# Second stages of the Hyena transforms as plain fp32 products, in a DeepNorm hybrid encoder layer

## The chip, the core and the metric

The kernel runs on one core of one Trainium2 chip. The metric is the device time of one execution in microseconds (us). The engines are TensorE (PE for matmuls, PEld for its weight loads), VectorE (DVE), ScalarE (ACT), GpSimd (POOL) and SyncE (SP, which here only issues DMAs). Each engine works through its own instructions in a fixed order and waits on semaphores.

## The reference

One post-norm layer over `x` of 1 x 1024 x 1024: an adaLN-modulated LayerNorm, one combined input projection of 9216 columns, then two branches, dilated window attention (512 channels) and a Hyena operator of order 2 (512 channels), gates, an output projection and a second LayerNorm. The change concerns the Hyena branch, whose core is this:

```python
def bidirectional_long_conv(z, h_fwd, h_bwd):
    L, C = h_fwd.shape
    circ = jnp.concatenate([h_fwd, jnp.zeros((1, C), jnp.float32), h_bwd[:0:-1]], axis=0)
    hf = jnp.fft.rfft(circ, axis=0)
    zf = jnp.fft.rfft(z.astype(jnp.float32), n=2 * L, axis=1)
    y = jnp.fft.irfft(zf * hf[None], n=2 * L, axis=1)[:, :L]
    return y.astype(z.dtype)
...
    z = v
    for o, gate_o in enumerate((x1, x2)):
        z = gate_o * (bidirectional_long_conv(z, filters[:, o, 0], filters[:, o, 1]) + filt_bias[o] * z)
    y_hy = z * jax.nn.silu(g_hy)
```

## The kernel before, in words

Everything is fp32 in meaning. Most matmuls use the faster type fp32r on operands split into a high and a low part, and add up three products: high by high, high by low, low by high. The input projection is the bulk of TensorE's work: `proj` (L234) splits one 1024 x 128 block of `w_in` into `wh` and `wl` (ACT at L222, POOL at L223) and runs 2 x 24 matmuls of 128x512 at L242 against the split input `hTh`, `hTl`. There are 64 such projections; those of the gates (`gate_r`, twelve of them "early") and of later channels serve as fill work on TensorE wherever the Hyena stages leave room.

The Hyena stages take the transform of length 2048 in two steps. `stage1` (L462) does butterflies over 16 residues on DVE with tiles of the ring `pair()` (tag `f`, seven buffers) and yields, one after the other, eight operands `y` of 128 x 2 x 256: `j = -1` for the two real residues and `j = 0..6` for the others. The second stage multiplies each `y` by a 128 x 128 table of cosines and one of sines; that is `split_product` (L492). It casts `y` to `yh` (ACT L499), forms the rest `yl` (DVE L500), writes negated copies of one half (ACT L511 and L512), and runs six fp32r matmuls of 128x512 at L521, with tables that are split as well; for `j = -1` in the filter stage twelve of 128x256 at L509:

```python
            ACT.copy(yh[:, c, :], y)
            V.tensor_tensor(yl[:, c, :], y, yh[:, c, :].bitcast(F32), ALU.subtract)
            ACT.mul(yh[:, n, :], y[:, at, :], -1.0)
            ACT.mul(yl[:, n, :], yl[:, 2 * at, :].bitcast(F32), -1.0)
            for k, (m, v) in enumerate(ops):
                PE.matmul(z, m, v, start=k == 0, stop=k == 5)
```

Two stages use it. `gen_filter` (L534) runs four times: eight blocks `g` of the filter in time (matmuls L560 and L561, times a decay table `dk` loaded at L556, product on DVE at L563), butterflies at L566 to L569, `stage1`, eight products with `tabf`, a copy by ACT (`hs`, L573, two buffers) and a DMA to `h_dram` (L581). `long_conv` (L615) also runs four times, under high priority: `stage1` of the data, eight forward products with `tcon` (j = -1: four fp32 matmuls with `tcon0` at L531, unsplit already), on DVE the product with the spectrum `ht` loaded from `h_dram` (`p1`, `p2` at L625 to L634), the inverse product, and butterflies back. `conv_to_rows` (L583) prepares its inputs: a projection, a width-3 convolution on DVE (L608) and eight transposes (L612).

A scheduler sets the order on each engine at build time, from dependencies, buffer counts and its own costs; on the chip the order is fixed. Buffers of one tile are in rings; a write waits until the ring's oldest buffer has been read. The right-hand pools `fl3` (with `tabf`) and, after it, `hy` and `hy2` (with `tcon`, `ht`) use the same memory one after the other.

Of the kernel before, what the change touches and what calls it, by code (L numbers as in the profile page):

```python
# [54 lines left out]
def _split(t):  # L55

    def r12(x):
        m, e = np.frexp(x)
        return np.ldexp(np.round(m * 4096) / 4096, e)

    h = r12(t)
    return h.astype(np.float32), r12(t - h).astype(np.float32)


def _dft_tables():

# [6 lines left out]
    flt = np.zeros((P, 36, P), np.float32)  # L73
    con = np.zeros((P, 28, P), np.float32)
    con0 = np.zeros((P, 8, P), np.float32)
    for n, j in enumerate(RES):
        m = b[:, None] * j + 16 * b[:, None] * k2[None, :]
        th = 2 * np.pi * (m % NB) / NB
        for i, t in enumerate((np.cos(th), np.sin(th))):
            flt[:, 4 * n + 2 * i], flt[:, 4 * n + 2 * i + 1] = _split(t)  # L80
        th = 2 * np.pi * ((m + j * k2[None, :]) % NB) / NB
        for i, t in enumerate((np.cos(th), np.sin(th))):
            con[:, 4 * n + 2 * i], con[:, 4 * n + 2 * i + 1] = _split(t)
    k = np.arange(64)
    alt = np.where(B_OF_P % 2 == 0, 1.0, -1.0)
    for i, k1 in enumerate((0, 8)):
# [8 lines left out]
        for m, (f, v) in enumerate(((c, ci), (sn, si))):  # L95
            t = 28 + 4 * m + 2 * i
            flt[:, t, rows], flt[:, t + 1, rows] = _split(f)
            con0[:, 2 * m + i, rows] = f
            con0[rows, 4 + 2 * i + m] = v.T
# [68 lines left out]
def hybrid_encoder(ctx, tc, A):  # L168
# [102 lines left out]
    with ExitStack() as st:  # L271
# [168 lines left out]
        tabf = fl3.tile([P, 36, P], F32R, name="tabf")  # L440
        PO.dma_start(tabf, A["t_flt"])
# [50 lines left out]
        def split_product(j, y, tab, inverse, pool):  # L492
# [3 lines left out]
            yh, yl = [pool.tile([P, 3, W], F32R, name="y" + q, tag="y" + q, bufs=2) for q in "hl"]  # L496
            at = int(inverse)
            c, n = slice(at, at + 2), 2 - 2 * at
            ACT.copy(yh[:, c, :], y)  # L499
            V.tensor_tensor(yl[:, c, :], y, yh[:, c, :].bitcast(F32), ALU.subtract)  # L500
            if j < 0:
                for i in range(2):
                    ops = []
                    for q in range(2):
                        t = 28 + 4 * i + 2 * q
                        for m, v in ((t, yh), (t, yl), (t + 1, yh)):
                            ops.append((tab[:, m, :], v[:, q, :]))
                    for k, (m, v) in enumerate(ops):
                        PE.matmul(z[:, i, :], m, v, start=k == 0, stop=k == 5)  # L509
                return z  # L510
            ACT.mul(yh[:, n, :], y[:, at, :], -1.0)  # L511
            ACT.mul(yl[:, n, :], yl[:, 2 * at, :].bitcast(F32), -1.0)  # L512
            ops = []
            for i, lo in ((0, at), (1, 1 - at)):
# [666 lines left out]
```

## Time and profile before

| | us |
|---|---|
| median of 3 runs (range) | 1463.67 (1461.36 to 1464.23) |
| the profiled execution | 1466.4 |
| its span, first to last instruction | 1464.6 |
| filter stage, first filter product to first product of a long convolution | 141.3 to 302.3 |
| four long convolutions, to the last inverse product | 302.3 to 613.9 |
| TensorE busy by the page | 1351.3 |
| VectorE busy | 957.6 |
| ScalarE busy | 624.4 |

The busy time of PE in the page counts the whole duration of each matmul, in which its neighbours overlap; how long TensorE is held by one matmul is read from the distance between two starts. A wait is charged to the instruction that waited and to the one that ended the wait. The rows come further down.

### The profile page before, as it was taken

To read this page: it belongs to the slowest core of one execution; us is meant where nothing else is said; L and a number is where in the kernel's file an instruction comes from. 1 tells how busy PE (TensorE), PEld (TensorE's weight loads), DVE (VectorE), ACT (ScalarE), POOL (GpSimd) and SP (SyncE) were. 2 spreads that over 40 slices of the span, in tenths; PEclk is the share of its full clock that TensorE was granted. 3 is DMA by queue.
4 is the path that set the end of the run, shared out by engine and by line. 5 is a ranking of instruction groups with operands and counts; after the bars stand their busy time and mean duration, and the time that the engine had idled before them with its cause. 6 is when DMAs were issued, how large, how long until landed. Compare 5 with 4: busy or idle time off the path is not lost.

```text
span 1464.6 us, 18389 instructions
## 1 busy us (share of the span) xinstructions
PE 1351.3 (92%) x6707; PEld 1098.4 (75%) x6707; DVE 957.6 (65%) x1709; ACT 624.4 (43%) x1220; POOL 282.2 (19%) x160
## 2 busy tenths in 40 slices
PE   4788979889899999999999999999999999689997
PEld 1467767767777777788988788878887888567886
DVE  4798768767999898745156714761466144288866
ACT  1544444534244443446355534663466343242110
POOL 1221121210113122141121112111211111231220
PEclk9799999999999999999999999999999999899999
DMA  9633544332112222121113421311131114588523
GB/s 255 182 97 105 175 133 149 110 130 79 54 58 69 87 65 79 58 84 30 44 59 116 103 61 58 92 30 43 59 91 31 44 58 123 184 249 220 158 88 72
DMA packets 157024, 145.86 MB, mean 100 GB/s; under 512 B 16611, under 2 KB 126591, under 8 KB 156678
## 3 DMA queue, kind: packets, MB, share of 16 engines
q1 hardware_dynamic: 156486, 140.44, 32.7%
q0 software_dynamic: 288, 4.19, 0.8%
q8 instruction: 53, 0.87, 0.3%
q14 instruction: 37, 0.30, 0.1%
q10 hardware_dynamic: 160, 0.06, 0.0%
HBM read 116.73 MB, written 27.92 MB: 99 GB/s over the span
## 4 chain that ended last, share of the span: by engine, by line
PE 64%; DVE 11%; DMA 5%; ACT 3%; issue 2%; POOL 1%; SPq 0%; DVEq 0%; ACTq 0%; POOLq 0%
PE pj L242 33%; PE pj L888 6%; PE z L521 6%; PE po L1138 6%; PE pj L1103 4%; PE po L929 2%; PE pp L922 2%; DVE iv L447 2%; DVE f L447 1%; DMA dk<-in_t_dec 1%; DMA wor<-in_w_out 1%; PE z L531 1%; PE ss L859 1%; DVE f L459 1%; DVE q L447 1%
## 5 line engine op out<-in xcount | busy, mean ns | idle before, releaser
L223 POOL TENSOR_TENSOR wl<-wr,wh 128x1024 fp32r<-128x1024 f32 x88 | 234.8, 2668 | 966.9 <-ACT wh L222 895.7
L242 PE MATMUL pj<-hTh,wh 128*128 128x512 f32 x1024 | 407.5, 398 | 4.0 <-ACT hTh L433 4.0
L242 PE MATMUL pj<-hTl,wh 128*128 128x512 f32 x1024 | 407.1, 398 | 1.5 <-POOL hTl L435 0.8
L242 PE MATMUL pj<-hTh,wl 128*128 128x512 f32 x1024 | 408.1, 399 | 0.0
L242 PEld LDWEIGHTS pj<-hTl,wh 128*128 128x128 f32 x1024 | 194.3, 190 | 40.5 <-DVE hTl L435 2.2
L242 PEld LDWEIGHTS pj<-hTh,wh 128*128 128x128 f32 x1024 | 194.4, 190 | 39.9 <-ACT hTh L433 4.1
L242 PEld LDWEIGHTS pj<-hTh,wl 128*128 128x128 f32 x1024 | 194.4, 190 | 37.3 <-issue 1.0
L222 ACT CAST wh<-wr 128x1024 fp32r<-128x1024 f32 x88 | 92.4, 1050 | 239.5 <-PE pj L242 82.3
L499 ACT CAST yh<-f 128x512 fp32r<-128x512 f32 x88 | 54.1, 615 | 105.2 <-DVE f L447 93.9
L899 DVE TENSOR_TENSOR tmp<-pj,bv 128x512 f32<-128x512 f32 x16 | 11.1, 692 | 115.0 <-PE pj L888 115.0
L500 DVE TENSOR_TENSOR yl<-f,yh 128x512 fp32r<-128x512 f32 x88 | 65.6, 756 | 22.2 <-ACT yh L499 19.9
L521 PE MATMUL z<-yh,tcon 128*128 128x512 f32 x224 | 65.7, 411 | 8.6 <-ACT yh L499 8.6
L918 ACT ACTIVATE sx<-sx,stat 128x256 f32<-128x256 f32 (+1 forms) x128 | 71.6, 563 | 3.1 <-DVE stat L916 3.0
L916 DVE CUSTOM_DVE_ANT_0 sx<-ss,tab 128x384 f32<-128x384 f32 (+1 forms) x112 | 53.7, 492 | 29.2 <-PE ss L844 18.0
L888 PE MATMUL pj<-wh,hTh 128*128 128x256 f32 x256 | 72.7, 284 | 0.0
L888 PE MATMUL pj<-wl,hTh 128*128 128x256 f32 x256 | 72.6, 284 | 0.0
L888 PE MATMUL pj<-wh,hTl 128*128 128x256 f32 x256 | 72.6, 284 | 0.0
L925 DVE TENSOR_TENSOR pt<-pp,pt 128x256 fp32r<-128x256 f32 (+1 forms) x128 | 61.8, 486 | 14.9 <-ACT pt L924 13.6
L1103 PE MATMUL pj<-yh,wl 128*128 128x512 f32 x128 | 52.0, 406 | 17.8 <-ACT yh L1084 11.3
L924 ACT CAST pt<-pp 128x256 fp32r<-128x256 f32 (+1 forms) x128 | 52.2, 425 | 33.4 <-PE po L929 28.9
L922 PE MATMUL pp<-ident,sx 128*128 128x128 f32 x320 | 58.3, 280 | 4.2 <-DVE pt L925 2.7
L521 PEld LDWEIGHTS z<-yh,tcon 128*128 128x128 f32 x224 | 40.6, 191 | 22.3 <-ACT yh L499 15.0
(236 smaller groups left out, 2546.2 us busy)
## 6 DMA issues: line engine op xcount, KB each, us to landing
wr<-in_w_in SPq DMA_DIRECT2D x64, 512.0 KB
xt<-in_x SPq DMA_DIRECT2D x32, 256.0 KB
wa<-in_w_ada SPq DMA_DIRECT2D x16, 512.0 KB
dk<-in_t_dec SPq DMA_DIRECT2D x32, 256.0 KB
r_d<-thr SPq DMA_DIRECT2D x32, 256.0 KB
h_dram<-hs SPq DMA_DIRECT2D x32, 256.0 KB
ht<-h_dram SPq DMA_DIRECT2D x32, 256.0 KB
thr<-r_d SPq DMA_DIRECT2D x32, 256.0 KB
```

The costliest lines, as they stand in the source:

```text
L222: ACT.copy(wh[:, :k, :], src)
L223: PO.tensor_tensor(wl[:, :k, :], src, wh[:, :k, :].bitcast(F32), ALU.subtract)
L242: PE.matmul(ps, w[:, kt, :], h[:, kt, sl], start=i == 0, stop=i == len(ops) - 1)
L447: V.tensor_tensor(o, a, b, op)
L500: V.tensor_tensor(yl[:, c, :], y, yh[:, c, :].bitcast(F32), ALU.subtract)
L521: PE.matmul(z, m, v, start=k == 0, stop=k == 5)
L888: PE.matmul(ps[:, t % 2], h[:, 4 * q + k, P * t : P * t + P], w[:, 2 * k : 2 * k + 2, :], start=first and t % 2 == 0 and i == 0, stop=last ...
L918: ACT.activation(sx[:, : n * P], sx[:, : n * P], AF.Exp, bias=stat[:, t, e, 0:1], scale=-1.0, accum_out=stat[:, t, e, 1:2])
L922: PE.transpose(pp[:, a * P : (a + 1) * P], sx[:, a * P : (a + 1) * P], ident)
L925: V.tensor_tensor(pt[:, :n, 1, :], blk(pp), pt[:, :n, 0, :].bitcast(F32), ALU.subtract)
L1103: PE.matmul(ps, w[:, 4 * b + kt, :], y[:, kt, :], start=i == 0, stop=i == len(ops) - 1)
L1138: PE.matmul(po, m[:, P * q : P * q + P], w[:, kt, ds_], start=n == 0, stop=n == 23)
```

## The change

`split_product` becomes `product`: `y` goes to TensorE as it is, in fp32, with unsplit tables, and the sine table is stored with both signs instead of negating a copy of `y`. For `j >= 0` that is one fp32 matmul of 128x512 (cosine) and two of 128x256 (sines, each on one half); for `j = -1` in the filter stage it is four of 128x256. The casts, the low parts and the negated copies go. The tables shrink from 36 and 28 blocks of 128 x 128 to 25 and 21, and SP issues their DMAs, not POOL. In the freed memory `ht` has two buffers, and `p1` and `p2` come from a ring `pr` of four, no longer from the ring `f`.

```diff
-        tabf = fl3.tile([P, 36, P], F32R, name="tabf")
-        PO.dma_start(tabf, A["t_flt"])
+        tabf = fl3.tile([P, 25, P], F32, name="tabf")
+        SY.dma_start(tabf, A["t_flt"])
...
-        def split_product(j, y, tab, inverse, pool):
+        def product(j, y, tab, inverse):
...
             z = ps_z.tile([P, 2, W], F32, name="z", tag="z")
-            yh, yl = [pool.tile([P, 3, W], F32R, name="y" + q, tag="y" + q, bufs=2) for q in "hl"]
-            at = int(inverse)
-            c, n = slice(at, at + 2), 2 - 2 * at
-            ACT.copy(yh[:, c, :], y)
-            V.tensor_tensor(yl[:, c, :], y, yh[:, c, :].bitcast(F32), ALU.subtract)
             if j < 0:
                 for i in range(2):
-                    ops = []
                     for q in range(2):
-                        t = 28 + 4 * i + 2 * q
-                        for m, v in ((t, yh), (t, yl), (t + 1, yh)):
-                            ops.append((tab[:, m, :], v[:, q, :]))
-                    for k, (m, v) in enumerate(ops):
-                        PE.matmul(z[:, i, :], m, v, start=k == 0, stop=k == 5)
+                        PE.matmul(z[:, i, :], tab[:, 21 + 2 * i + q, :], y[:, q, :], start=q == 0, stop=q == 1)
                 return z
-            ACT.mul(yh[:, n, :], y[:, at, :], -1.0)
-            ACT.mul(yl[:, n, :], yl[:, 2 * at, :].bitcast(F32), -1.0)
-            ops = []
-            for i, lo in ((0, at), (1, 1 - at)):
-                t = 4 * j + 2 * i
-                for m, v in ((t, yh), (t + 1, yh)):
-                    ops.append((tab[:, m, :], v[:, lo : lo + 2, :]))
-            for i, lo in ((0, at), (1, 1 - at)):
-                ops.append((tab[:, 4 * j + 2 * i, :], yl[:, lo : lo + 2, :]))
-            for k, (m, v) in enumerate(ops):
-                PE.matmul(z, m, v, start=k == 0, stop=k == 5)
+            PE.matmul(z, tab[:, 3 * j, :], y, start=True, stop=False)
+            for i in range(2):
+                t = 3 * j + 1 + (i ^ int(inverse))
+                PE.matmul(z[:, i, :], tab[:, t, :], y[:, 1 - i, :], start=False, stop=i == 1)
             return z
...
-                ht = hy2.tile([P, 2, W], F32, name="ht", tag="ht", bufs=1)
+                ht = hy2.tile([P, 2, W], F32, name="ht", tag="ht", bufs=2)
                 SY.dma_start(ht, h_dram[hc, o, :, j + 1])
                 z = conv_product(j, y, False)
-                p1, p2 = pair(), pair()
+                p1, p2 = [hy2.tile([P, 2, W], F32, name="pr", tag="pr", bufs=4) for _ in range(2)]
...
-        tcon = hy.tile([P, 28, P], F32R, name="tcon")
-        PO.dma_start(tcon, A["t_con"])
+        tcon = hy.tile([P, 21, P], F32, name="tcon")
+        SY.dma_start(tcon, A["t_con"])
```

The scheduler makes a new order of it. On TensorE, in the first long convolution, the order before around the inverse product of j = -1 and the forward product of j = 0 (`tcon_2263` is `tcon0`, `tcon` the split table, L242 a fill matmul):

```order
L531 MATMUL z<-f,tcon_2263 128x256
L242 MATMUL pj<-hTh,wl 128x512
L242 MATMUL pj<-hTh,wh 128x512
L531 MATMUL z<-f,tcon_2263 128x256 x3
L521 MATMUL z<-yh,tcon 128x512 x4
L521 MATMUL z<-yl,tcon 128x512 x2
L242 MATMUL pj<-hTl,wh 128x512
```

and now (`tcon_1963` is `tcon0`, `pr` holds the spectral product, L228 is the fill):

```order
L500 MATMUL z<-pr,tcon_1963 128x256
L487 MATMUL z<-f,tcon 128x512
L500 MATMUL z<-pr,tcon_1963 128x256 x3
L490 MATMUL z<-f,tcon 128x256 x2
L228 MATMUL pj<-hTl,wh 128x512
```

The six fp32r matmuls of the forward product have become one of 512 and two of 256 columns, which read `f` directly.

The second place on TensorE is the end of the last filter's products. Before, fill stands between them and the low parts come last (`tabf` is the split table, L612 transposes of `conv_to_rows`):

```order
L521 MATMUL z<-yh,tabf 128x512 x2
L242 MATMUL pj<-hTl,wh 128x512
L521 MATMUL z<-yh,tabf 128x512 x2
L521 MATMUL z<-yl,tabf 128x512
L521 MATMUL z<-yh,tabf 128x512
L521 MATMUL z<-yl,tabf 128x512
L521 MATMUL z<-yh,tabf 128x512 x3
L242 MATMUL pj<-hTh,wl 128x512
L521 MATMUL z<-yl,tabf 128x512
L612 MATMUL px<-ident,y 128x128
L521 MATMUL z<-yl,tabf 128x512
```

Now the products stand in pairs of rows, one behind the other, and fill follows them:

```order
L487 MATMUL z<-f,tabf 128x512
L490 MATMUL z<-f,tabf 128x256 x2
L487 MATMUL z<-f,tabf 128x512
L490 MATMUL z<-f,tabf 128x256 x2
L228 MATMUL pj<-hTh,wl 128x512
```

Fill matmuls moved as a whole. Counted in the two orders between the marks (3072 in all in both):

| fill matmuls of 128x512 | before | now |
|---|---|---|
| ahead of the first filter product | 225 | 221 |
| from there to the first product of a long convolution (filters 1 to 4, and behind them) | 93, 77, 82, 24, 31 | 65, 54, 54, 1, 42 |
| long convolutions 1 to 3, each up to the next one's first product | 211, 210, 215 | 173, 208, 157 |
| of those, between a convolution's last product and the next one's first | 76, 76, 80 | 81, 119, 74 |
| long convolution 4, up to its last product | 138 | 90 |
| behind that | 1766 | 2007 |

On SP, where the last filter's spectra go out (L581), the first spectrum for the convolution comes in (`ht`, L622, `h_2289`, L630) and `tcon0` follows, the order before was:

```order
L581 DMA h_dram<-hs 128x512 [waits DMAHW3_49,Activation_49]
L622 DMA ht<-h_dram 128x512 [waits DMAHW4_49,DMASW0_49,PE_49]
L630 DMA h_2289<-h_dram 128x256 [waits DMAHW5_49]
L731 DMA tcon_2263<-in_t_con 128x1024 [waits DMAHW6_49,DVE_49]
L229 DMA wr<-in_w_in 128x8x128 [waits DMAHW7_49,Pool_49]
```

with `tcon` on POOL's queue beside it; now it is:

```order
L550 DMA h_dram<-hs 128x512 [waits DMAHW0_49,Activation_49]
L591 DMA ht<-h_dram 128x512 [waits DMAHW1_49,PE_49]
L599 DMA h_1989<-h_dram 128x256 [waits DMAHW2_49,PE_49]
L591 DMA ht<-h_dram 128x512 [waits DMAHW3_49]
L252 DMA r_d<-thr 128x512 [waits DMAHW4_49,Activation_49]
L700 DMA tcon_1963<-in_t_con 128x1024 [waits DMAHW5_49,DVE_49]
L702 DMA tcon<-in_t_con 128x2688 [waits DMAHW7_49,DMAHW6_49]
L252 DMA r_d<-thr 128x512 [waits Activation_49]
```

`tcon` (21 blocks) has moved behind `tcon0` onto SP's queue, behind a second `ht` and a store of gate values (L252), which waits for ACT.

## Rows read from the trace of the kernel before

**Rows 1.** The page, its first part: busy time of each engine, share of the span, number of instructions.

```profile
PE 1351.3 (92%) x6707; PEld 1098.4 (75%) x6707; DVE 957.6 (65%) x1709; ACT 624.4 (43%) x1220; POOL 282.2 (19%) x160
```

**Rows 2.** Busy time by stretch. Columns: stretch and its length in us, then busy us and number of instructions of PE, PEld, DVE, ACT and POOL, the granted clock of TensorE as a share of the full one, share of the DMA engines' time, GB/s. The first is the filter stage; then come the four long convolutions, each with its products and, for the first three, the part behind the last product up to the next one's first.

```profile
141.30:302.30 161.00, 140.32 (x635) 112.15 (x636) 121.65 (x180) 74.78 (x149) 32.85 (x20) 0.94 0.45 147
302.30:365.10 62.80, 59.50 (x244) 46.77 (x245) 44.38 (x79) 26.10 (x55) 4.85 (x2) 0.94 0.24 76
365.10:386.60 21.50, 17.30 (x78) 13.97 (x76) 21.34 (x30) 5.21 (x6) 7.24 (x2) 0.95 0.20 62
386.60:452.90 66.30, 63.93 (x276) 50.78 (x277) 57.11 (x108) 32.92 (x65) 7.31 (x3) 0.96 0.19 58
452.90:468.10 15.20, 13.47 (x61) 10.84 (x59) 15.20 (x26) 2.32 (x3) 9.62 (x1) 1.00 0.09 35
468.10:530.50 62.40, 58.61 (x267) 46.16 (x268) 52.48 (x93) 31.15 (x64) 7.32 (x3) 1.00 0.28 87
530.50:551.00 20.50, 18.50 (x82) 14.96 (x81) 20.07 (x31) 5.69 (x7) 7.17 (x2) 1.00 0.16 52
551.00:613.90 62.90, 59.83 (x247) 45.63 (x248) 49.09 (x83) 28.71 (x59) 10.44 (x4) 0.97 0.23 72
```

**Rows 3.** Groups of PE's instructions from 141.3 to 613.9, each shape apart. Columns: line, engine, operation, out<-in, shapes, number | busy us, mean ns of one | idle us before them and what ended it. An fp32 matmul leaves two records, an fp32r one leaves one.

```profile
L242 PE MATMUL pj<-hTl,wh 128*128 128x512 f32 x361 | 143.4, 397 | 0.0
...
L521 PE MATMUL z<-yh,tcon 128*128 128x512 f32 x224 | 65.7, 411 | 8.6 <-ACT yh L499 8.6
L521 PE MATMUL z<-yl,tcon 128*128 128x512 f32 x112 | 41.3, 418 | 3.7 <-DVE yl L500 3.7
L521 PE MATMUL z<-yh,tabf 128*128 128x512 f32 x112 | 37.7, 438 | 6.9 <-ACT yh L499 6.9
L531 PE MATMUL z<-f,tcon 128*128 128x256 f32 x64 | 20.9, 473 | 13.2 <-DVE f L447 8.0 <-DMA tcon<-in_t_con 5.1
```

**Rows 4.** Timeline of PE in a run of 22 fill matmuls without a gap: start us, duration us, engine, line, operation, number.

```profile
292.10 0.39 PE L242 MATMUL pj<-hTh,wh 128*128 128x512 f32 x1
...
296.86 0.39 PE L242 MATMUL pj<-hTh,wh 128*128 128x512 f32 x1
```

**Rows 5.** Timeline of the weight loads PEld around the first inverse product of j = -1 (three fp32 matmuls of 256 columns, six records) and the first forward product of j = 0 (six fp32r matmuls of 512).

```profile
309.57 1.28 PEld L531 LDWEIGHTS z<-f,tcon 128*128 128x128 f32 x6
...
310.88 0.86 PEld L521 LDWEIGHTS z<-yh,tcon 128*128 128x128 f32 x4
...
312.25 0.19 PEld L242 LDWEIGHTS pj<-hTl,wh 128*128 128x128 f32 x1
```

**Rows 6.** Timeline of PE at the two fp32 matmuls of 512 columns of the gate (four records of 0.59 us each).

```profile
864.52 1.88 PE L950 MATMUL pg<-acc,ones 128*1 128x512 f32 x4
866.33 0.39 PE L888 MATMUL pj<-wh,hTh 128*128 128x256 f32 x1
```

**Rows 7.** The chain of waits up to 640 us, in order of time: ten of the twelve fp32r matmuls of 256 columns of one filter product of j = -1.

```profile
267.12 1.15 PE z L509 x10
```

**Rows 8.** Groups on DVE in the long convolutions (columns as in rows 3).

```profile
L500 DVE TENSOR_TENSOR yl<-f,yh 128x512 fp32r<-128x512 f32 x56 | 43.7, 788 | 12.7 <-ACT yh L499 10.7
...
L625 DVE TENSOR_TENSOR f<-z,ht 128x512 f32<-128x512 f32 x32 | 22.0, 689 | 29.8 <-PE z L521 22.1 <-PE z L531 7.5
```

**Rows 9.** The same on ACT in the long convolutions.

```profile
L499 ACT CAST yh<-f 128x512 fp32r<-128x512 f32 x56 | 34.5, 615 | 92.7 <-DVE f L447 83.1 <-DVE f L459 9.4
L512 ACT ACTIVATE yl<-yl 128x256 fp32r<-128x256 f32 x56 | 23.2, 416 | 14.4 <-DVE yl L500 13.9
```

**Rows 10.** Waits of PE from 120 to 300 us: who waited for whom, us in total, times, the longest.

```profile
PE z L521 <- ACT yh L499: 6.9, 2, 3.7
PE z L509 <- ACT yh L499: 6.6, 4, 2.0
```

**Rows 11.** The same from 300 to 620 us.

```profile
PE z L521 <- ACT yh L499: 8.6, 6, 1.9
PE z L531 <- DVE f L447: 8.0, 3, 4.2
PE z L531 <- DMA tcon<-in_t_con: 5.1, 1, 5.1
```

**Rows 12.** Timeline in the first long convolution: a split of fill weights on POOL, the DVE operation beside it, and the product behind.

```profile
345.07 2.46 POOL L223 TENSOR_TENSOR wl<-wr,wh 128x1024 fp32r<-128x1024 f32 x1 [16.28 <-ACT wh L222]
345.20 2.88 DVE L459 SCALAR_TENSOR_TENSOR f<-q 128x512 f32<-128x512 f32 x1
...
348.34 0.68 DVE L459 SCALAR_TENSOR_TENSOR f<-f 128x512 f32<-128x512 f32 x1
...
349.18 0.50 PE L521 MATMUL z<-yh,tcon 128*128 128x512 f32 x1 [1.91 <-ACT yh L499]
```

**Rows 13.** Timeline of DVE between the first and the second long convolution.

```profile
380.55 4.42 DVE L447 TENSOR_TENSOR q<-xx 128x1024 f32<-128x1024 f32 x2
```

**Rows 14.** Timeline of DVE in the second filter: first and last block of `g`, and the butterfly whose result is the operand of j = -1.

```profile
164.13 1.29 DVE L563 TENSOR_TENSOR g<-px,dk 128x512 f32<-128x512 f32 x2 [3.83 <-PE px L561]
...
176.94 0.69 DVE L563 TENSOR_TENSOR g<-px,dk 128x512 f32<-128x512 f32 x1 [0.74 <-DMA dk<-in_t_dec]
...
185.37 0.75 DVE L447 TENSOR_TENSOR f<-f 128x256 f32<-128x256 f32 x2
```

More of the change, by code (lines that the diff above doesn't have):

```diff
@@ L52 @@
 HIGH = 20000
[L55 to L62, printed above, removed]
 def _dft_tables():
@@ L72, in _dft_tables @@
     k2 = b
-    flt = np.zeros((P, 36, P), np.float32)
-    con = np.zeros((P, 28, P), np.float32)
+    flt = np.zeros((P, 25, P), np.float32)
+    con = np.zeros((P, 21, P), np.float32)
     con0 = np.zeros((P, 8, P), np.float32)
@@ L78, in _dft_tables @@
         th = 2 * np.pi * (m % NB) / NB
-        for i, t in enumerate((np.cos(th), np.sin(th))):
-            flt[:, 4 * n + 2 * i], flt[:, 4 * n + 2 * i + 1] = _split(t)
+        flt[:, 3 * n], flt[:, 3 * n + 1], flt[:, 3 * n + 2] = np.cos(th), np.sin(th), -np.sin(th)
         th = 2 * np.pi * ((m + j * k2[None, :]) % NB) / NB
-        for i, t in enumerate((np.cos(th), np.sin(th))):
-            con[:, 4 * n + 2 * i], con[:, 4 * n + 2 * i + 1] = _split(t)
+        con[:, 3 * n], con[:, 3 * n + 1], con[:, 3 * n + 2] = np.cos(th), np.sin(th), -np.sin(th)
     k = np.arange(64)
@@ L95, in _dft_tables @@
         for m, (f, v) in enumerate(((c, ci), (sn, si))):
-            t = 28 + 4 * m + 2 * i
-            flt[:, t, rows], flt[:, t + 1, rows] = _split(f)
+            flt[:, 21 + 2 * m + i, rows] = f
             con0[:, 2 * m + i, rows] = f
@@ L525, in conv_product @@
             if j >= 0:
-                return split_product(j, y, tcon, inverse, hy2)
+                return product(j, y, tcon, inverse)
             z = ps_z.tile([P, 2, W], F32, name="z", tag="z")
@@ L570, in gen_filter @@
             for j, y in stage1(u, g[:, 8:12], g, g[:, 12:16], u, g[:, 8:12]):
-                z = split_product(j, y, tabf, False, fl3)
+                z = product(j, y, tabf, False)
                 hs = fl3.tile([P, 2, W], F32, name="hs", tag="hs", bufs=2)
```

## The prediction

> **What bounds the kernel now.** I read the page first, then the busy time by stretch, the groups by shape, the timeline, and the waits of PE. The page puts PE at 92% and DVE at 65% [rows 1], but the busy time of a matmul overlaps its neighbours', so I count by distance between starts. A fill matmul holds TensorE for (296.86 - 292.10) / 21 = 0.2267 us [rows 4]. Six fp32r matmuls of a product hold it from 310.88 to 312.25, 1.37 us, 0.229 each [rows 5]; fp32r matmuls of 256 columns take 1.15 / 10 = 0.115 [rows 7], and I use that for the small ones (96 at L560 and L561) and 0.11 for the transposes.
>
> The change lies in the stretch from 141.3 to 613.9, 472.6 us [rows 2]. What TensorE has to do in it at full clock: 1081 fill matmuls by the table of the change (245.1 us), 504 at L521 (115.4), 48 at L509 (5.5), 32 fp32 matmuls at L531 as 64 records of 0.218 (14.0) (the numbers of both lines [rows 3]), 96 small ones (11.0), 88 transposes (9.7): 400.7 us. So 72 us are lost there, 34.6 in the filter stage and 37.3 in the long convolutions: waits, stretches at the lower clock (the mean granted clock is 0.94 in the filter stage and in the first convolution [rows 2]) and short stalls. The reader is to see that this is all the room there is. PE's waits name ACT's cast for 6.9 and 6.6 us in the filters [rows 10], and for 8.6 us in the convolutions, DVE's butterflies for 8.0 and the table's DMA for 5.1 [rows 11]. DVE is nearly as full: in the four product stretches it is busy for 44.4 of 62.8, 57.1 of 66.3, 52.5 of 62.4 and 49.1 of 62.9 us, and in what lies between them almost all the time [rows 2].
>
> **The change part by part.** *Products.* An fp32 matmul of 256 columns is two records, six of which run from 309.57 to 310.88: 0.218 per record, 0.436 per matmul [rows 5]. One of 512 columns is two records as well; four take 1.88 us of which the last lasts 0.59, so (1.88 - 0.59) / 3 = 0.43 each, 0.86 per matmul [rows 6]. A new product is then 0.86 + 2 x 0.436 = 1.73 us against 1.37, 0.36 more. There are 84 (28 in the filters, 56 in the convolutions): 30.2 us. The four of j = -1 in the filters go from 12 x 0.115 = 1.38 to 4 x 0.436 = 1.74: 1.4 us. TensorE gets 31.6 us of new work. No row has an fp32 matmul of 512 columns with a full table; the nearest is the gate's with one column of weights. Below it lies nothing, since its stream is the same; above, a first record as long as the 0.59 us that a record lasts would make the product 0.16 us longer, 14 us in all. I take 0.86 and keep both ends.
>
> The Trainium skill has two rules for this. "FP8 and Floating Point Precision", TensorE Precision Notes, says that true fp32 makes four passes; "Perfetto Trace Analysis", Engine Utilization, halves the output rate for fp32 in low and high parts. A record of 0.218 us for 256 columns, two records to a matmul, is a quarter of the fp32r rate, so the trace stands with the first; by the second the product would cost about half, which is a rival below.
>
> *Casts and splits.* DVE loses 56 operations of 0.788 us in the convolutions (43.7 us [rows 8]) and 32 in the filters; ACT loses the cast of 0.615 us and two negations of 0.416 per product [rows 9]. None of that is TensorE's time. What it gives is a shorter chain into each product: the butterfly's result goes straight to PE, without cast (0.62), split (0.69) and negation (0.42), and DVE has about 11 us less to do in each convolution. It pays only as far as PE's 72 lost us shrink.
>
> *Filter stage.* In the second filter the eight blocks `g` take from 164.1 to 177.6, 13.5 us, paced by the loads of `dk`, and 8.5 us more go by until the operand of j = -1 is there, at 186.1 [rows 14]. The change touches neither. The products then stand back to back: eight times 1.73 is 13.8 us, against 13 DVE operations of 512 columns (0.68 each [rows 12]), one of twice and four of half that size that feed them, some 11 us; with 0.5 us for the start, 14.3. The next `g` needs its matmuls behind these. A filter is thus 36.3 us, three of them 109; the last has 15.3 us to the end of its products, and 42 fill matmuls (9.5 us, I take 10) cover the wait for `tcon0`. The stage becomes 134 us, against 161.0: 27 less.
>
> *Long convolutions.* By the table, fill inside the product stretches falls from 135, 134, 135, 138 to 92, 89, 83, 90. (The first four come from 211 - 76, 210 - 76, 215 - 80 and 138.) With products, j = -1 and transposes TensorE's work in these is now 49.5, 48.8, 48.3 and 49.0 us, 195.6 in all; before it was 54.2, 55.7, 56.8 and 54.9, 221.6, and took 254.4 [rows 2], so 8.2 us were lost in each. How much of that stays is the open question. What stays for certain is DVE held by POOL: while POOL splits fill weights from 345.07 on for 2.46 us, a DVE operation that else takes 0.68 takes 2.88, and PE waits 1.91 us for what follows it [rows 12]; between the convolutions two butterflies take 4.42 us in the same way [rows 13]. Also PE now has 11 to 13 fill matmuls, 2.5 to 2.9 us, between a forward and its inverse product, and DVE's four operations in between need about 2.1 (two of 0.69 [rows 8], two of half the size), so a held DVE shows at once. What goes is ACT's part. Bounds: 8.2 each if every wait only changes its name, 2 each if only the short stalls stay. I take 6, nearer the first, because the collisions are in the rows and the hop over ACT is about 1 us of each wait: 195.6 + 24 = 219.6. Between the convolutions 81, 119 and 74 fill matmuls (and transposes) are 18.4, 28.7 and 17.7 us of TensorE; DVE's own chain was 21.5 and 20.5 in the first and third [rows 2], so I take 20.5, 28.7 and 20: 69.2. Together 288.8 us, against 311.6.
>
> *What is moved.* The stretch gets shorter by 472.6 - 134.2 - 288.8 = 49.6 us, but 241 fill matmuls have left its front and middle and stand behind the last convolution, where TensorE is packed: 241 x 0.2267 = 54.6 us. The four fewer ahead of the first filter give 0.9 back.
>
> *Tables and queues.* `tcon` waited on nothing but the freed memory and held PE for 5.1 us behind `tcon0` [rows 11]; now it queues on SP behind `tcon0`, two spectra and a store that waits for ACT's gate values of the fill just before. I count the 5.1 us as covered by the 42 fill matmuls; if the store is late it stays, 5 us worse. `tabf` on SP waits for tiles of the first stage and stands ahead of small weights and `dk`; if it held the next fill weights, a few us. The second `ht` buffer and the ring `pr` cost nothing and I give them nothing: DVE at `p1` waited 22.1 and 7.5 us for PE's products and never for a spectrum [rows 8].
>
> *Sum.* -49.6 + 54.6 - 0.9 = +4.1 us on a span of 1464.6, in an execution of 1466.4, 2.7 us above the median of 1463.67. On the median: 1468 us, 0.3% slower.
>
> **The rivals.** *A: every wait only changes its name.* The 72 us stay lost and the new work adds in full: 1464 + 32 = 1495, or a little more. For it: TensorE is the fullest engine, and the wait of rows 12 begins at a DVE operation that POOL holds. Against: 6.9 and 6.6 us of the filters' waits end at ACT's cast, which goes. *B, the other side: the chain over three engines was what kept TensorE waiting.* Place: the product stretches and the filter products. Without it, and with DVE about 11 us freer per convolution, the losses of 8.2 us per product stretch fall to 3 (21 us more than before instead of 9) and the lower clock, which follows the long waits, is granted less. Then 40 to 47 of the 72 us go, and the time is 1464 + 31.6 - 45 = 1450. It decides from 31.6 us regained on; for faster by a measurable amount, 34.5. My own sum regains 27.5, so the two are not far apart. For it: PE's waits for the cast; against it, rows 12. *C: half price.* If an fp32 product cost 0.86 us, as the halved rate would have it, TensorE would lose 84 x 0.51 = 43 us of work instead of gaining 30, and with the waits of my own forecast the time would be 1464 - 43 - 27 = 1394. Rows 5 and 6 speak against it. *D: no change,* between the forecast and B, some 30 us regained: 1464.
>
> **How the numbers follow.** A measurement of this kernel can tell 0.2%, about 3 us, from no change. Chances: my forecast (slower by 3 to 20 us) 0.38, A 0.10, D 0.22, B 0.28, C 0.02. Slower 0.48, same 0.22, faster 0.30. The likeliest case's own range is 1467 to 1484. The range of 8 in 10 reaches from B's middle to a loss of 22 us: 1448 to 1486; it leaves out the far part of B, C and most of A.
>
> **What would show it.** In the trace after: per product six records, two of about 0.43 and four of about 0.218 us, 1.73 in all; no operation at the casts; the distance from one filter's first product to the next at about 36 us; the four product stretches at about 55 us each with DVE near 40; waits of PE for DVE alone, next to a split on POOL; the first long convolution starting without a wait for the table's DMA; and behind the last convolution some 55 us more of fill. The forecast is wrong on the fast side if filters come at 32 us or the stretches at 51, and on the slow side if PE waits at fp32 products on something other than DVE, or if a record of 512 columns takes more than 0.45 us.

## The result, and the profile after

The changed kernel takes 1483.35 us in the median of its first four runs (1472.47 to 1484.12) beside 1462.51 of the kernel before: the ratio is 1.0126, interval 1.0090 to 1.0162. In a second set of six runs it was 1475.23 (1470.74 to 1481.29) beside 1460.59, ratio 1.0111 (1.0086 to 1.0136). It is 16 to 18 us slower where the prediction had 4. One kernel's runs spread over 10 to 20 us, so differences below 5 us are read from ratios with their intervals only. The profiled execution of after is 1483.17 us with a span of 1481.4, 16.8 more than before.

The page's busy time of PE, to be set beside [rows 1]: 26 us more, while ACT lost 102 and DVE 61.

```profile
PE 1377.2 (93%) x6691; PEld 1101.5 (74%) x6691; DVE 896.3 (61%) x1621; ACT 521.9 (35%) x964; POOL 287.0 (19%) x158
```

The busy time by stretch in after (columns as in [rows 2]): filter stage, then the four long convolutions with what lies between them, then the part behind the last product up to the first attention score.

```profile
140.90:279.80 138.90, 125.35 (x520) 93.04 (x521) 96.33 (x144) 32.37 (x52) 28.80 (x17) 0.96 0.46 152
279.80:333.90 54.10, 51.99 (x201) 37.89 (x201) 33.93 (x64) 9.56 (x15) 7.35 (x3) 0.97 0.24 78
333.90:354.60 20.70, 18.61 (x83) 15.06 (x81) 20.36 (x33) 4.05 (x5) 6.52 (x2) 1.00 0.28 88
354.60:407.30 52.70, 51.17 (x198) 37.44 (x198) 33.93 (x65) 8.06 (x12) 4.99 (x2) 0.97 0.26 78
407.30:442.10 34.80, 30.32 (x136) 24.91 (x135) 27.83 (x46) 9.82 (x13) 5.10 (x2) 0.95 0.11 31
442.10:495.80 53.70, 51.08 (x201) 36.84 (x200) 39.25 (x76) 11.19 (x16) 6.10 (x2) 0.97 0.22 67
495.80:515.90 20.10, 17.91 (x83) 14.56 (x82) 19.74 (x31) 5.12 (x7) 8.05 (x2) 1.00 0.12 39
515.90:570.10 54.20, 51.37 (x199) 37.57 (x199) 38.25 (x69) 9.39 (x13) 9.31 (x3) 0.97 0.22 73
570.10:671.90 101.80, 99.89 (x456) 82.56 (x456) 36.23 (x59) 32.02 (x43) 26.52 (x18) 1.00 0.24 75
```

The part behind the last product in the kernel before:

```profile
613.90:657.10 43.20, 43.20 (x199) 35.42 (x199) 24.98 (x43) 16.33 (x22) 16.61 (x13) 1.00 0.27 82
```

The filter stage fell from 161.0 to 138.9 us, the convolutions from 311.6 to 290.3, and what stands behind them grew from 43.2 to 101.8: together 15.2 us more, at a DVE that is busy for 34 to 39 us of each product stretch instead of 44 to 57.

One inverse and one forward product, timeline of PE (start, duration, engine, line, operation, records). From 294.27 to 295.99 is 1.72 us: 0.86 for the 512 columns, 0.86 for the two sines. The forecast was 1.73.

```profile
294.27 1.02 PE L487 MATMUL z<-pr,tcon 128*128 128x512 f32 x2
295.13 1.03 PE L490 MATMUL z<-pr,tcon 128*128 128x256 f32 x4
295.99 1.02 PE L487 MATMUL z<-f,tcon 128*128 128x512 f32 x2
296.85 0.81 PE L490 MATMUL z<-f,tcon 128*128 128x256 f32 x3
```

That is 0.43 us a record of 512 columns, nearly four fill matmuls (0.2267) to an fp32 one: the four passes that the Trainium skill names in "FP8 and Floating Point Precision", TensorE Precision Notes, and not the halved rate of "Perfetto Trace Analysis", Engine Utilization.

The waits of PE in the convolutions of after (who for whom, us, times, longest), to be set beside [rows 11]: the cast is gone, of the 5.1 us for the table's DMA 0.3 are left, and the rest is DVE.

```profile
PE z L487 <- DVE pr L433: 6.3, 4, 1.9
PE px L581 <- DVE y L577: 4.5, 1, 4.5
PE z L500 <- DVE f L433: 4.3, 2, 2.2
PE z L500 <- DVE pr L433: 2.7, 2, 2.0
PE z L500 <- DMA tcon<-in_t_con: 0.3, 1, 0.3
```

Two of these in the timeline. First the 4.5 us between the second and the third convolution: the order puts the transposes of `conv_to_rows` at a place where DVE has just begun the eight operations on `y` that they need, behind the butterflies. The stretch took 34.8 us for 28.5 us of TensorE's work.

```profile
422.90 5.42 DVE L577 SCALAR_TENSOR_TENSOR y<-u,cols,y 128x768 f32<-128x768 f32 x8
...
423.45 0.39 PE L228 MATMUL pj<-hTh,wl 128*128 128x512 f32 x1
...
428.32 1.09 PE L581 MATMUL px<-ident,y 128*128 128x128 f32 x4 [4.48 <-DVE y L577]
```

Second, in the third convolution, the collision of [rows 12] again: two operations of 256 columns, for which DVE takes 0.87 us alone (at 464.90), take 2.96 while POOL splits, and the inverse product comes 1.9 us late. Of the eight waits for DVE in front of products, four end beside a split on POOL or within 0.7 us of its end (at 446.88, 474.29, 515.90 and 568.34); two (375.36 and 548.39) have no split in the 5 us before them.

```profile
471.18 2.96 DVE L433 TENSOR_TENSOR pr<-pr 128x256 f32<-128x256 f32 x2
...
471.50 2.36 POOL L209 TENSOR_TENSOR wl<-wr,wh 128x1024 fp32r<-128x1024 f32 x1 [24.96 <-ACT wh L208]
...
474.29 1.10 PE L487 MATMUL z<-pr,tcon 128*128 128x512 f32 x2 [1.94 <-DVE pr L433]
```

### The profile page after: what moved, and what is told of

Same layout as the page of the kernel before. It is cut to its first block, busy times and chain, and to the rows that moved or that the text cites. A ratio compares the mean times of both kernels' runs of the same rounds, so it can differ in the third digit from the quotient of the medians.

```text
span 1481.4 us, 17997 instructions
## 1 busy us (share of the span) xinstructions
PE 1377.2 (93%) x6691; PEld 1101.5 (74%) x6691; DVE 896.3 (61%) x1621; ACT 521.9 (35%) x964; POOL 287.0 (19%) x158
## 4 chain that ended last, share of the span: by engine, by line
PE 64%; DVE 11%; DMA 4%; issue 2%; ACT 2%; POOL 1%; SPq 0%; DVEq 0%; ACTq 0%; POOLq 0%
PE pj L228 33%; PE pj L857 6%; PE po L1107 6%; PE pj L1072 4%; PE z L487 3%; PE z L490 3%; PE po L898 2%; DVE iv L433 2%; PE pp L891 2%; DMA wor<-in_w_out 1%; DVE y L577 1%; PE z L500 1%; DVE q L433 1%; PE ss L828 1%; DVE iv L445 1%
## 5 line engine op out<-in xcount | busy, mean ns | idle before, releaser
L228 PE MATMUL pj<-hTh,wh 128*128 128x512 f32 x1024 | 408.5, 399 | 4.8 <-ACT hTh L419 4.8
L228 PE MATMUL pj<-hTl,wh 128*128 128x512 f32 x1024 | 407.9, 399 | 1.2 <-POOL hTl L421 0.7
L228 PE MATMUL pj<-hTh,wl 128*128 128x512 f32 x1024 | 408.8, 399 | 0.0
L228 PEld LDWEIGHTS pj<-hTh,wh 128*128 128x128 f32 x1024 | 194.3, 190 | 41.0 <-ACT hTh L419 5.1
L228 PEld LDWEIGHTS pj<-hTl,wh 128*128 128x128 f32 x1024 | 194.2, 190 | 39.8 <-DVE hTl L421 1.6
L228 PEld LDWEIGHTS pj<-hTh,wl 128*128 128x128 f32 x1024 | 194.1, 190 | 37.5 <-issue 1.2
L885 DVE CUSTOM_DVE_ANT_0 sx<-ss,tab 128x384 f32<-128x384 f32 (+1 forms) x112 | 53.7, 493 | 29.0 <-PE ss L813 18.1
L894 DVE TENSOR_TENSOR pt<-pp,pt 128x256 fp32r<-128x256 f32 (+1 forms) x128 | 61.8, 486 | 14.9 <-ACT pt L893 13.6
L1072 PE MATMUL pj<-yh,wl 128*128 128x512 f32 x128 | 53.2, 416 | 17.2 <-ACT yh L1053 11.6
L577 DVE SCALAR_TENSOR_TENSOR y<-u,cols,y 128x56 f32<-128x56 f32 (+2 forms) x96 | 52.4, 592 | 10.2 <-ACT y L565 10.2
L898 PE MATMUL po<-pt,v 128*128 128x256 f32 x320 | 55.6, 294 | 0.3
L891 PEld LDWEIGHTS pp<-ident,sx 128*128 128x128 f32 x320 | 36.9, 140 | 24.1 <-ACT sx L887 8.6
L1107 PE MATMUL po<-woh,ml 128*128 128x512 f32 (+1 forms) x136 | 51.3, 377 | 1.8 <-DVE ml L1077 1.8
```

The costliest lines, as they stand in the source:

```text
L228: PE.matmul(ps, w[:, kt, :], h[:, kt, sl], start=i == 0, stop=i == len(ops) - 1)
L577: V.scalar_tensor_tensor(a, b, w[k], a, ALU.mult, ALU.add)
L885: V.tensor_tensor_reduce(blk(sx), blk(ss), tabs(t), scale=-(2.0 ** (-h - 4)), scalar=3e38, op0=ALU.add, op1=ALU.min, accum_out=stat[:, t, ...
L891: PE.transpose(pp[:, a * P : (a + 1) * P], sx[:, a * P : (a + 1) * P], ident)
L894: V.tensor_tensor(pt[:, :n, 1, :], blk(pp), pt[:, :n, 0, :].bitcast(F32), ALU.subtract)
L898: PE.matmul(po[:, t % 2], v[:, 2 * e : 2 * e + 2, :], pt[:, a], start=a == 0, stop=a == n - 1)
```

## The experiments

In this table "lost" is the length of a stretch less TensorE's work in it, with durations read from starts in the traces (0.2267 us for a fill matmul, 0.43 and 0.2157 for the new records, 0.119 for 256 columns, 0.109 for a transpose; slightly other values than in the prediction, whose sum for before is 72), so waits and time at the lower clock are in it. "Work" is TensorE's work against the kernel before. Each row is from one profiled execution; medians and ratios are from all runs, beside runs of the kernel before on the same chip.

| kernel | work, us | lost: filters | convolutions | behind | sum | median, us | ratio to before (interval) |
|---|---|---|---|---|---|---|---|
| before | 0 | 34.5 | 38.0 | 0.4 | 72.9 | 1460 to 1463 | 1 |
| changed | +31.6 | 22.6 | 30.8 | 2.4 | 55.8 | 1483.4 | 1.0126 (1.0090 to 1.0162) |
| changed, again | +31.6 | 22.9 | 30.8 | 2.5 | 56.2 | 1475.2 | 1.0111 (1.0086 to 1.0136) |
| one sine less | -5.0 | 29.3 | 26.4 | 6.1 | 61.8 | 1443.8 | 0.9891 (0.9856 to 0.9926) |
| filters only | +11.5 | 25.0 | 45.0 | 0.1 | 70.1 | 1470.9 | 1.0092 (1.0059 to 1.0126) |
| convolutions only | +20.2 | 29.6 | 26.7 | 0.2 | 56.5 | 1467.4 | 1.0054 (1.0026 to 1.0083) |
| no buffers | +31.6 | 21.2 | 26.3 | 0.2 | 47.7 | 1470.6 | 1.0084 (1.0054 to 1.0114) |
| more fill | +31.6 | 26.2 | 23.7 | 1.7 | 51.6 | 1474.7 | 1.0109 (1.0083 to 1.0135) |
| before, more fill | 0 | 34.4 | 44.9 | 11.6 | 90.9 | 1481.0 | 1.0138 (1.0114 to 1.0163) |
| all splits on DVE | +31.6 | 26.3 | 12.1 | 0.4 | 38.8 | 1464.8 | 1.0026 (0.9998 to 1.0053) |
| before, splits on DVE | 0 | 25.9 | 18.0 | 12.1 | 56.1 | 1448.6 | 0.9914 (0.9891 to 0.9938) |
| changed, splits on DVE | +31.6 | 20.1 | 18.4 | 0.6 | 39.1 | 1468.8 | 1.0056 (1.0034 to 1.0079) |
| the same, no buffers | +31.6 | 22.2 | 5.0 | 0.2 | 27.4 | 1449.4 | 0.9926 (0.9901 to 0.9951) |
| convolutions only, splits on DVE | +20.2 | 25.3 | 14.4 | 0.2 | 39.9 | 1448.6 | 0.9925 (0.9900 to 0.9949) |

Work plus the change of the sum of losses gives each kernel's distance from before to within 7 us, but for one: "changed, splits on DVE" is 8 us above before where the ledger has it 2 below; its profiled execution, at 1462.0, was the fastest of its seven, 6.8 us under its median.

**The changed kernel again** (no edit). 

> The changed kernel once more, beside its own runs of before. If the 1.26% stands: 15 to 21 us above before. If one of its first four runs (11 us below the others) was the usual one: about 10 us above.

Measured: 1.0111, 16.2 us. The first result stands, and the single run of 1472 us lies within the spread.

**What TensorE's work is worth.** The sine matmul of the second half of each product is left out.

```diff
-            for i in range(2):
+            for i in range(1):
```

> The changed kernel without the sine matmul of the second half of each product (its output is left incomplete): 84 x 0.436 = 36.6 us less for TensorE, so 5 us less than in the kernel before, and the same chain over DVE and ACT as in the changed kernel. Theory (TensorE's work decides, waits grow a little as it gets shorter): 1483 - 36.6 plus up to 8, 1447 to 1455. Rival (DVE's chain decides in the products): the stretches stay, 1470 to 1480.

Measured: 1443.8, 31 us below the changed kernel of the second set for 36.6 us of work, a little under the expected 1447 to 1455. The rival falls: the product stretches follow TensorE's work at once. The busy time of the first and the last of them (columns as in [rows 2]):

```profile
276.20:322.60 46.40, 44.47 (x178) 31.57 (x178) 36.59 (x72) 11.53 (x16) 5.02 (x2) 1.00 0.32 99
...
491.00:537.80 46.80, 44.82 (x178) 31.22 (x178) 39.22 (x74) 10.34 (x15) 9.17 (x3) 1.00 0.28 90
```

46.4 and 46.8 us against 54.1 and 54.2: 7.4 to 7.7 less, for 14 x 0.436 = 6.1 of matmul. Fill and transposes in them nearly balance; the rest is lost time that went too (the granted clock is 1.00 in both, where it was 0.97).

**One stage at a time.** `product` for the filters with `split_product` left in the convolutions, without the buffers; and the reverse, with them.

```diff
-                z = split_product(j, y, tabf, False, fl3)
+                z = product(j, y, tabf, False)
...
                 return split_product(j, y, tcon, inverse, hy2)
```

> Only the filters' 32 products are fp32; the long convolutions split as before, with their own buffers. Theory (TensorE's work, less the waits that come back in the same stage): 28 x 0.36 + 1.4 = 11.5 us more work, and 34.4 - 22.7 = 11.7 us of waits gone in the filter stage, as in the changed kernel: 1462 us, between 1457 and 1468. Rival (both stages cost alike, 18 us over 84 products): 28/84 of it, 1469. Rival (the shorter chain is the gain and the convolutions spoil it): under 1455.

> Only the 56 products of the long convolutions are fp32, with the second spectrum buffer and the ring; the filters split as before. Theory: 56 x 0.36 = 20.2 us more work, 7.2 us of waits back in the convolutions, up to 5 us given back behind them and at the end: 1476 to 1481. Rival (both stages cost alike): 56/84 of 18 us, 1475. Rival (the convolutions' part pays, the filters spoil it): 1462 or less.

Measured: 1470.9 and 1467.4, both misses of my theory, in opposite directions; the first lies next to its rival's 1469, the second under its rival's 1475, so an equal cost per product doesn't fit either. The losses don't stay in their stage. With the filters alone in fp32 the filter stage gave back 9.5 us of the 11.7 expected, but the convolutions, whose code is that of before, lost 7 more. The first of them again waited for its table, which the table counts with the filters:

```profile
PE z L544 <- DMA tcon<-in_t_con: 6.4, 1, 6.4
```

With the convolutions alone in fp32 more came back than in the changed kernel: 11.3 us in them. The price of a product is the same (1.72 us from 138.15 to 139.87 in the filters-only run); what comes back depends on the whole order of the instructions, and can't be added up stage by stage.

**The buffers.** One spectrum buffer and the ring `f` for the spectral products, in the changed kernel.

```diff
-                ht = hy2.tile([P, 2, W], F32, name="ht", tag="ht", bufs=2)
+                ht = hy2.tile([P, 2, W], F32, name="ht", tag="ht", bufs=1)
...
-                p1, p2 = [hy2.tile([P, 2, W], F32, name="pr", tag="pr", bufs=4) for _ in range(2)]
+                p1, p2 = pair(), pair()
```

> The changed kernel with one spectrum buffer again and the spectral products in the common ring. Theory (DVE never waited for a spectrum): within 4 us of the changed kernel, 1479 to 1487. Rival (the buffers are what shortens the convolutions' stretches): each of the four gets up to 3.8 us longer, 1490 to 1498. Rival (more freedom let the order go wrong): 1470 or less.

Measured: 1470.6, outside the theory's 1479 to 1487 and next to the third rival's 1470. Against before it is 1.0084 where the changed kernel has 1.0111 and 1.0126: below them, but the intervals overlap. With the splits on DVE (below) the same edit was tried again, and there it is clear.

**Fill, released earlier.** Two more projections of fill ahead of the third filter, in the changed kernel and in the one before.

```diff
-GATES = (0, 3, 2)
+GATES = (2, 3, 2)
```

> The changed kernel with two more projections of fill released ahead of the third filter: by the order, 322 fill matmuls instead of 216 stand in the filter stage, and 97 fewer behind the convolutions. Theory (TensorE loses 22.6 us in the filter stage since no fill is left to put there): the stage grows by less than the 24 us that the fill takes, 8 to 16 us come back, 8 to 16 us below the changed kernel. Rival (TensorE waits in front of the products, where the order puts no fill): the stage grows by the full 24 us, within 4 us of the changed kernel. Rival (the spectra come later and the chain of DVE ends last): slower.

> The same edit in the kernel before, where the order moves 34 fill matmuls (7.7 us) into the filter stage. Theory: with enough fill already there, within 5 us of before. Rival (any kernel with this edit gains): 8 us or more below before, and then the gain of the changed kernel with it says nothing on the change.

Measured: 1.0109, level with the changed kernel, and 1.0138, 20 us slower than before, which neither expectation had. In the changed kernel the filter stage grew by 27.7 us for 24 us of fill, the first rival:

```profile
136.50:303.10 166.60, 148.89 (x626) 111.45 (x626) 99.19 (x140) 37.22 (x58) 35.71 (x19) 0.98 0.43 140
```

So TensorE stands idle there in front of products (8.6 us for DVE's `f`, 3.3 us for ACT's copy `hs`), not for lack of fill. In the kernel before, the convolutions lost 7 us more, and 11 us went behind the last one, where the fill was now missing; the busy time of that part, and PE's wait in it:

```profile
635.10:679.30 44.20, 35.71 (x154) 28.93 (x154) 23.09 (x43) 13.91 (x19) 11.07 (x12) 0.88 0.22 70
```

```profile
PE px L705 <- DVE xx L693: 8.3, 3, 4.5
```

The gate's transposes wait there for DVE's last butterflies, as only 135 fill matmuls stand in this part, where before had 182 and lost nothing; and its granted clock is 0.88 in the mean of the part. Fill kept in store for that place is worth 11 us here.

**DVE held by POOL.** The splits of the fill weights go to DVE: first all that are asked for from the first filter on (26 in the trace), and then only those asked for from the end of the fourth filter to the last convolution (21).

```diff
-        PO.tensor_tensor(wl[:, :k, :], src, wh[:, :k, :].bitcast(F32), ALU.subtract)
+        (V if on_dve[0] else PO).tensor_tensor(wl[:, :k, :], src, wh[:, :k, :].bitcast(F32), ALU.subtract)
```

> The changed kernel with the splits of the fill weights on DVE instead of POOL, from the first filter to the last convolution. Theory (POOL's splits hold DVE, and the products wait for it): the 31 us lost in the convolutions fall by 8 to 15, 8 to 15 us below the changed kernel. Rival (DVE's own chain is what counts, and each split adds about 1.1 us to it): 5 to 20 us above the changed kernel.

Measured: 1464.8, 10 us below the changed kernel beside it; the two intervals don't touch. The busy time of the last three convolutions (POOL idle, the second and third at 50.1 and 49.9 us where they were 52.7 and 53.7):

```profile
354.60:404.70 50.10, 50.10 (x199) 37.16 (x199) 32.72 (x63) 8.78 (x13) 0.00 (x0) 1.00 0.27 82
...
434.30:484.20 49.90, 49.90 (x206) 36.96 (x206) 38.41 (x78) 10.17 (x15) 0.00 (x0) 1.00 0.26 77
...
502.90:553.90 51.00, 46.49 (x173) 32.45 (x174) 40.05 (x77) 8.69 (x12) 0.00 (x0) 0.97 0.27 83
```

The butterflies on the spectral products in after, and then here: 496 ns in the mean with POOL beside them, 419 without (columns as in [rows 3]).

```profile
L433 DVE TENSOR_TENSOR pr<-pr 128x256 f32<-128x256 f32 x64 | 31.8, 496 | 0.6
```

```profile
L435 DVE TENSOR_TENSOR pr<-pr 128x256 f32<-128x256 f32 x64 | 26.8, 419 | 0.4
```

The Trainium skill says in "SBUF — State Buffer", Who interferes with whom, that a DVE instruction with two inputs in SBUF contends with a GpSimd instruction that reads SBUF, over a pair of ports that is locked for one of them. The trace agrees: the operation of [rows 12] ends 0.55 us behind POOL's split, the two at 471.18 end 0.28 us behind theirs.

> The kernel before, with the splits of those fill weights that are asked for between the fourth filter and the last convolution on DVE instead of POOL (21 of them). Theory (the gain of this edit needs the room that the change made on DVE): the 21 splits of about 1.1 us lengthen DVE's chain by what the collisions cost it, within 5 us of before. Rival (POOL holding DVE costs both kernels the same): 8 to 13 us below before, about 1450.

Measured: 1448.6, 0.9914: the rival. POOL's hold on DVE costs the kernel before 11.5 us too, though DVE there gets 21 splits of 1.22 us on top:

```profile
L225 DVE TENSOR_TENSOR wl<-wr,wh 128x1024 fp32r<-128x1024 f32 x21 | 25.7, 1222 | 5.6 <-issue 3.8 <-ACT wh L224 1.7
```

The edit also changes the order (135 fill matmuls stand behind the convolutions instead of 182), so the 11.5 us belong to the edit; that the hold alone makes them is argued from the rows, not shown. As both kernels gain alike, it doesn't explain the difference between them.

> The same edit in the changed kernel (16 splits). Theory (what was left of the waits in the convolutions was DVE held by POOL): the loss in the convolutions falls from 31 us to under 15, 1457 to 1465, level with before or a little under it. Rival (the gain of the run with all splits on DVE came from the filter stage): above 1470.

> As the one before it, with one spectrum buffer and the spectral products in the common ring (18 splits). Theory (the buffers give nothing): within 4 us of it. Rival (the ring lets products run ahead): 5 us or more above it. Rival (it only lets the order push more fill behind the convolutions): 4 to 8 us below it.

Measured: 1468.8 and 1449.4, and no run of the one is as fast as any of the other (1462.0 to 1470.8; 1444.4 to 1452.9). The first missed its 1457 to 1465, though the loss in the convolutions fell to 18.4 us; of the second's expectations the last had the direction, at 4 to 8 us. Both have 21 splits on DVE in the trace. The second spectrum buffer and the ring cost 19 us here; the two profiled executions are 11.4 us apart, which the table's losses account for (39.1 against 27.4), and the other 8 us are in no trace. The first kernel, second convolution, the gap behind it, and the fourth; then its waits:

```profile
342.50:391.70 49.20, 49.20 (x196) 36.35 (x195) 32.02 (x61) 7.09 (x10) 0.00 (x0) 1.00 0.28 83
391.70:420.90 29.20, 24.81 (x111) 20.20 (x109) 25.64 (x48) 9.13 (x12) 0.00 (x0) 0.94 0.13 36
...
487.90:538.40 50.50, 43.81 (x165) 30.82 (x165) 37.64 (x70) 5.82 (x9) 0.00 (x0) 0.97 0.27 84
```

```profile
PE z L489 <- DVE pr L435: 4.8, 2, 2.4
PE px L583 <- DVE y L579: 4.4, 1, 4.4
PE z L502 <- DVE pr L435: 1.9, 1, 1.9
```

The second, the same stretches and its waits:

```profile
349.10:403.40 54.30, 54.28 (x220) 40.16 (x221) 36.23 (x71) 9.99 (x14) 0.00 (x0) 1.00 0.27 85
403.40:426.50 23.10, 22.97 (x105) 18.70 (x104) 22.57 (x40) 7.42 (x9) 0.00 (x0) 1.00 0.16 45
...
497.20:551.60 54.40, 54.36 (x222) 40.17 (x223) 42.55 (x83) 11.72 (x16) 0.00 (x0) 1.00 0.28 87
```

```profile
PE z L502 <- DVE f L435: 1.2, 1, 1.2
PE z L502 <- DVE q L435: 0.9, 1, 0.9
```

Without the buffers 432 fill matmuls lie in the four product stretches, with them 335. A stretch is longer without them (54.3 and 54.4 us against 49.2 and 50.5), but TensorE is busy in all of it, where in the fourth stretch with them it is busy for 43.8 of 50.5. The transposes again wait 4.4 us for `y` with the buffers and not at all without. What the waits name is DVE in both; what differs is the order.

> Filters split as before, fp32 products in the convolutions alone, and the splits of fill weights on DVE there (16). Theory (each stage pays 0.36 us a product and gets its own waits back; in the convolutions more than that once POOL no longer holds DVE): 3 to 8 us under the run with both stages in fp32, 1450 to 1458, under both kernels. Rival (the filters' products pay for themselves): level with it.

Measured: 1448.6, 20 us under the run with both stages in fp32, where 3 to 8 were expected. It is below both kernels, as expected, by 0.75%, but so are two others, and the three can't be told apart. Here the buffers are in and only the filters are split, so it isn't the buffers as such that cost 19 us, but the order that they make together with the fp32 filters. Which of the two buffers does it was not tried.

## Why the prediction was right or wrong

*Direction and bound: right.* TensorE's work decides, it grew by the forecast amount, and the waits did not give it back. That is borne out by the sine run (31 us for 36.6 of work). The size was not: 16 to 18 us instead of 4, inside the case's own range only because that went up to 20.

*Products: right.* 1.72 us against 1.73; the first record of 512 columns was not longer.

*Filter stage: 138.9 us against 134.2.* The step that failed is "the products then stand back to back", taken at 14.3 us a filter and 15.3 in the last. They took 15.9, 16.0, 16.2 and 16.1, 6 us more, which is more than the whole error; the rest of the three distances, 22.0 in the forecast, was 24.5, 21.3 and 19.1 (distances of 40.4, 37.3 and 35.3 instead of 36.3), and 9.9 us led to `tcon0` (forecast 10). In the first two filters PE waits inside the products until ACT has copied a `z`; in the second, ACT's copy `hs` waits for one of its two buffers to be stored:

```profile
191.19 1.26 ACT L542 ACTIVATE hs<-z 128x512 f32<-128x512 f32 x2 [5.67 <-DMA h_dram<-hs]
191.84 1.13 PE L487 MATMUL z<-f,tabf 128*128 128x512 f32 x2 [1.45 <-ACT hs L542]
```

ACT's waits for that store in the filter stage, before and now:

```profile
ACT hs L573 <- DMA h_dram<-hs: 9.3, 2, 5.1
ACT hs L542 <- DMA h_dram<-hs: 27.3, 12, 5.7
```

So the store behind the products, which the forecast left out, now reaches PE, which stands 2.3 us for `hs` in the stage and stood none before. The sign for the slow side (PE waiting at fp32 products for something other than DVE) was there; a third buffer of `hs` was not tried. In the last two filters the product of j = -1 ran at the lower clock, most of its records 0.43 us apart instead of 0.2157, which cost 1.8 and 1.6 us, after PE had stood 2.5 us for DVE (the granted clock was 0.63 from 218.5 to 222 us and 0.51 from 254 to 257):

```profile
253.86 3.48 PE L485 MATMUL z<-f,tabf 128*128 128x256 f32 x8 [2.50 <-DVE f L433]
```

In the first distance, DVE stood 7.7 us before the first `g`, for matmuls that came behind the transposes of another operand and 2.0 us later still, until ACT had copied these:

```profile
159.85 0.39 PE L529 MATMUL px<-w4h,hid 128*128 128x256 f32 x1 [1.99 <-ACT xx L582]
160.63 1.29 DVE L532 TENSOR_TENSOR g<-px,dk 128x512 f32<-128x512 f32 x2 [7.74 <-PE px L530]
```

*Long convolutions: 290.3 against 288.8, by two errors.* The product stretches lost 4.1 to 5.6 us each where I took 6, 214.7 us in all against 219.6; rows 12 was the right guide for about half of it, since what was left there were waits for DVE alone, but only four of the eight stand next to a split on POOL. What lies between them took 75.6 against 69.2, nearly all of it in the second, 34.8 against 28.7. There I took TensorE's work as the time, as if it could not wait, and the transposes waited 4.5 us for `y`.

*What is moved: 58.6 us against 54.6.* The fill came behind as counted (54.6). With it came 16 transposes of `conv_to_rows`, 1.7 us that my sum did not move, and a wait in front of them for DVE's convolution:

```profile
584.91 1.06 PE L581 MATMUL px<-ident,y 128*128 128x128 f32 x8 [1.91 <-DVE y L577]
```

"TensorE is packed there" held for the kernel before only.

*The rest.* Early -0.4 (forecast -0.9), attention -0.8, and the end +2.7. That last is no part of the change: in the second profile of the changed kernel the end took 194.2 us, before 196.3.

*Buffers: "cost nothing and I give them nothing" was wrong.* That DVE never waits for a spectrum was read rightly, but the order that is made with the buffers holds less fill in the stretches. I take it that a free buffer lets the planner put the next product ahead; that is not shown. With the splits on DVE the order with the buffers costs 19 us. With them on POOL, as in the change, the ratios are 1.0084 without and 1.0111 to 1.0126 with the buffers, so the 4 to 6 us that this would make are likely and not shown.

So the 16.8 us of the profiled pair are 31.6 of work, less 17.1 of losses given back, with the end's 2.7 on top and 1.2 off early and in the attention: 16.0, and 0.8 that the rounding of the durations leaves. My sum had 27.5 given back; the 10 us that are missing are in the three places named. Rival B, on the other side, needed 31.6 back. In the changed kernel without buffers and with the splits on DVE 45 came back, and it is level with the kernel before that has the same splits (0.9926 and 0.9914), which itself lost 12 us behind its convolutions: with those two hindrances gone, the fp32 products cost about what they give, as long as the other kernel keeps these 12.

What stays open: why the filters in fp32 and the buffers together make an order that loses so much; why runs of one kernel spread over 10 us and more (the part ahead of the first filter alone took 132 to 146 us in the fourteen profiles, of different kernels); and whether the 12 us lost behind the convolutions in the kernel before with splits on DVE could be had by keeping more fill for that place, which was not tried.

## What to carry to other kernels

Where the fullest engine gets new work, its price could be read here from single records (31.6 us forecast and found); what a shorter chain gives back could not, and it didn't stay in the stage where the chain was. When a chain gets shorter, look also at what stands behind it: here the store of the result became the next wait. Where a planner sets the order, a buffer that nothing waits for is still a change, because it changes the order: try it by itself. And an elementwise operation on POOL can be paid for by DVE: moving the splits to DVE was worth 0.9% in the kernel before, nearly as much as the whole change cost.

## What was not expected of the hardware

A split of 128x1024 took 2.36 us on POOL (3.42 in the mean of the 14 in the convolutions of after, with DVE beside it) and 1.22 on DVE, and while it ran on POOL two DVE operations that take 0.87 us together took 2.96. So DVE got off with less when it did POOL's work itself, even where it is as full as in the kernel before (44 to 57 us of each product stretch of 62 to 66): 21 splits of 1.22 us more, and the four convolutions were 13 us shorter (298.6 against 311.6). The factor of two between the engines is also what the Trainium skill gives in "GPSIMD Engine Reference", Elementwise — side-by-side cycle accounting, for an add of 2048 elements. TensorE's granted clock fell to 0.88 in the stretch behind the last convolution when fill ran out there, and was 1.00 in the same stretch of before.
